# Gate matrices of an expert layer traced between the activations ahead of the value steps

## The chip, the cores and the metric

The kernel runs on one core of one Trainium2 chip. The metric is device time in microseconds (us) of one execution; several executions are timed and their median is given. In this document PE is TensorE, DVE is VectorE, ACT is ScalarE, POOL is GpSimd and SP is the engine whose queue issues most loads.

## The reference

Two layers work on 256 latent tokens and 256 context tokens of width 1024. Layer 0 mixes the tokens by a bidirectional mLSTM beside windowed attention, layer 1 by gated linear attention. After each mixer comes a retrieval layer over 128 x 128 = 16384 single-neuron experts, and the change is inside that layer:

```python
def block(hb):                                     # hb: 128 tokens
    q = (hb @ wq).reshape(tc, 8, 2, 128)
    s = jnp.einsum('thpk,hpnk->thpn', q, keys)
    s_top, i_top = lax.top_k(s, 16)
    cand = s_top[:, :, 0, :, None] + s_top[:, :, 1, None, :]
    cid = i_top[:, :, 0, :, None] * 128 + i_top[:, :, 1, None, :]
    best, pos = lax.top_k(cand.reshape(tc, 8, -1), 16)
    eid = jnp.take_along_axis(cid.reshape(tc, 8, -1), pos, -1)
    g = jax.nn.softmax(best, -1)
    act = jax.nn.gelu(jnp.einsum('td,thed->the', hb, u[eid]))
    return jnp.einsum('the,thed->td', g * act, v[eid])
```

Each token so has 8 x 16 = 128 chosen experts with a weight (gate) each. Layer 0 runs this for 512 tokens, layer 1 for the 256 latent tokens.

## The kernel before

**The expert layer is computed densely.** For a tile of 128 tokens the kernel does not gather rows of `u` and `v`; it multiplies the tokens with all 16384 rows of `u`, multiplies the result by a matrix of gates that is zero for experts that were not chosen, and multiplies that with all rows of `v`. (One of layer 0's four tiles goes the other way, by indirect loads on POOL's queue, during the value steps.) Layer 0 has three dense tiles (384 tokens), layer 1 two (256 tokens).

**Stages of a dense layer.** `top16` takes the 16 best keys of each head and finds the 16 best pairs; a `lookup` on DVE (tiles `rge`, `rpr`, `rsf`) turns their positions into two indices, and the three rows of `rabg` hold the first index, the second index and the gate of 128 slots per token. `slots` transposes them on PE (`abgT`) and ACT copies the result to `iT` and `gT`. `expand` builds the gate matrix of 8 tokens at a time (a group): DVE writes `oa` (first index equal to a counter), `eq` (second index equal to it) and two products `ob` (`eq` times the gate in two half-precision parts), PE multiplies `oa` by `ob` (16 matmuls in two PSUM tiles `G`), ACT copies `G` into `stg`, and after two groups ACT's queue writes 1 MB of `stg` to DRAM. A tile has 16 groups, so layer 0 has 48 and layer 1 has 32.

`stream` is the rest. Step n of the activations (`u_step`, 64 of them) has two halves; each loads 512 KB of `u`, splits it into a high part `uhi` (ACT, line 140) and a low part `ulo` (line 141, on POOL when the argument `n` of `halves` is true, else on DVE), does 24 matmuls on PE and takes a GELU on ACT (`act`, line 880). Step n of the values (`v_step`) loads gates back (`gin`), multiplies them into `act`, splits the product (`wh`, `wl`) and two blocks of `v`, and accumulates in PSUM (`F`). Layer 0 computes 32 activation steps ahead of the first value step, layer 1 computes 23; these are the early steps, and in them all low halves are POOL's.

**What sets the order.** A tile scheduler places the instructions of every engine's queue from the order in which the Python code creates them and from the buffers: three each of `uhi` and `ulo`, five loads (`wt`), three each of `oa` and `eq`, four of `ob`, six PSUM banks for `G`, two for `u`, two of `stg`, and one `rabg`. Queues run in order. In the code before, all groups of all tiles are created ahead of `stream`. The transposes of `slots` alone are pinned by a table: tile i's stand on PE behind the activation step that `TURNS` names (line 31).

```python
TURNS = ((10, 13, 17), (7, 17))
            w = self.halves(self.I["u"][l, 2 * n + j], [P, KD, P], early or (2 * n + j) % 3 == 2, "u")
                for tt in range(2):
                    self.expand(self.slots(self.top16(route[tt])), gd, tt, count)
```

Of the kernel before, what the change touches and what calls it, by code (L numbers as in the profile page):

```python
# [9 lines left out]
F32 = mybir.dt.float32  # L10
# [10 lines left out]
P = 128  # L21
D = 1024
KD = 8
T = 256
# [3 lines left out]

STARTS = [0, 16, 24, 29, 34, 37, 40, 43] + list(range(46, 54))

TURNS = ((10, 13, 17), (7, 17))
NCAND = 54
GS = 2.0 ** 15

TG = 16
OT = 8
CH = 8
TD = 384
# [66 lines left out]
class Kernel:  # L105
# [609 lines left out]
    def top16(self, route):  # L715

        nc, pp = self.nc, self.pp
# [25 lines left out]
            nc.vector.max_index(Px[:, h, 8:16], B[:, h, 8:16], C[:, h])  # L743
        pos = pp.tile([P, P], BF, name="rpos")
        nc.vector.tensor_copy(pos, Px.rearrange("t h k -> t (h k)"))
        abg = pp.tile([P, 3, P], F32, name="rabg")
        sf = pp.tile([P, P], BF, name="rsf")
        H = P // 2

# [48 lines left out]
    def expand(self, slots, gd, tt, count):  # L798

        nc = self.nc
        ix, gate = slots

        g = self.pp.tile([P, 2, P], F16, name="gpair")
        nc.vector.tensor_scalar(g[:, 0], gate, GS, None, op0=OP.mult)
        nc.vector.scalar_tensor_tensor(g[:, 1], gate, GS, g[:, 0], op0=OP.mult, op1=OP.subtract)
        for tg in range(P // TG):
            stg = self.sb("stg", [P, P, TG], "stg")
            for o in range(TG // OT):  # L810
                t0 = tg * TG + OT * o
                shape = [P, OT // 2, P, 2]
                oa = self.sb("s2a", shape, "oa", F16)
                eq = self.sb("s2b", shape, "eq", F16)
                ob = self.sb("rows", [P, 2] + shape[1:], "ob", F16)

                def each(x):
                    return x[:, t0:t0 + OT].rearrange("p (a t) -> p a t", t=2)[:, :, None, :].to_broadcast(shape)
                iota = count[:, None].to_broadcast(shape)
                nc.vector.tensor_tensor(oa, iota, each(ix[:, 0]), op=OP.is_equal)  # L820
                nc.vector.tensor_tensor(eq, iota, each(ix[:, 1]), op=OP.is_equal)  # L821
                for h in range(2):
                    nc.vector.tensor_tensor(ob[:, h], eq, each(g[:, h]), op=OP.mult)  # L823
                for j in range(OT // 4):
                    ps = self.bank([P, 4, P], "G")
                    for i in range(4):
                        a, t = divmod(4 * j + i, 2)
                        self.mm(ps[:, i], oa[:, a, :, t], ob[:, 0, a, :, t], True, False)
                        self.mm(ps[:, i], oa[:, a, :, t], ob[:, 1, a, :, t], False, True)
                    c = OT * o + 4 * j  # L830
                    nc.scalar.copy(stg[:, :, c:c + 4].rearrange("p i t -> p t i"), ps)  # L831
            nc.scalar.dma_start(gd[:, :, tt * (P // TG) + tg].rearrange("b p c t -> p b (c t)"),
                                stg.rearrange("p (b c) t -> p b (c t)", c=CH))

    def gather_start(self, abg):

# [34 lines left out]
    def u_step(self, l, n, c0, nt, early):  # L871

        nc = self.nc
        a = self.sb("ring", [P, 2, nt], "act")
        for j in range(2):
            w = self.halves(self.I["u"][l, 2 * n + j], [P, KD, P], early or (2 * n + j) % 3 == 2, "u")
            ps = self.bank([P, nt], "u", "u")
            for k in range(KD):
                i = self.mm3(ps, [x[:, k] for x in w], self.hcols(k, c0, nt), k == 0, k == KD - 1)
            nc.scalar.activation(a[:, j], ps, AF.Gelu)  # L880

        for t, tile_no in self.turns:
            if TURNS[l][tile_no] == n:
                self.tc.add_manual_dep(t, i.ins.name, mybir.DependencyInfo(
                    mybir.DependencyClass.NoSync, mybir.DependencyReason.DATA), reason="issue order")
        return a
# [32 lines left out]
                self.mm(F[tt][hf], w[:, j, ts], b[:, hf * 512:hf * 512 + 512],  # L919
                        first and w is wh and b is hi, last and w is wl)  # L920

    def stream(self, l, gd, c0, nt, ahead, spill, side=None):


        nc = self.nc
# [3 lines left out]
            order += [("u", x), ("v", x - ahead + spill)]  # L929
        order += [("v", y) for y in range(64 - ahead + spill, 64)]  # L930
        acts, far = {}, {}
        for i, (what, n) in enumerate(order):
            if what == "u":
                a = self.u_step(l, n, c0, nt, n < ahead)
                if n < spill:
# [377 lines left out]
    def run(self):  # L1313
# [4 lines left out]
        with self.banks("S"):  # L1318
            with self.open("S"):
                F = self.experts0()  # L1320
# [3 lines left out]
        with self.banks("S"):  # L1324
            with self.open("S2"):
                gd = self.pd.tile([P // CH, P, T // TG, CH, TG], F32, name="G1")
# [1 line left out]
                weave((self.route(1, "l", route), 16))  # L1328
                self.turns, self.tile_no = [], 0
                count = self.count()  # L1330
                for tt in range(2):
                    self.expand(self.slots(self.top16(route[tt])), gd, tt, count)
                mods = self.seq(self.modulation(1, 5, (0,), "stg"), self.last_rows(xd["l"]))
                F = self.stream(1, gd, T, T, 23, 0, lambda x: x >= 35 and x % 8 == 3 and next(mods, None))
                self.last_norm(F)

    def experts0(self):
# [3 lines left out]
        route = []  # L1341
# [2 lines left out]
        gst = self.gst = self.gather_start(self.top16(self.route_c[0]))  # L1344
        slots = [self.slots(self.top16(r)) for r in self.route_c[1:] + route]
        count = self.count()
        for tt in range(3):
            self.expand(slots[tt], gd, tt, count)
        gst["f"] = self.sb("fa", [P, D], "fa")
        nc.gpsimd.memset(gst["f"], 0.0)  # L1350
        gst["rows"], done, far, spill = {}, [0, 0], 4, 28
# [3 lines left out]
        def side(x):  # L1355
# [7 lines left out]
            while done[1] < goal:  # L1363
# [2 lines left out]
                    done[0] += 1  # L1366
                self.gather_use(gst, done[1])
                done[1] += 1
        return self.stream(0, gd, P, TD, 32, spill, side)

    def mixers(self, xd):
        nc, pw, I = self.nc, self.pw, self.I
# [156 lines left out]
```

## Time and profile before

| what | value |
|---|---|
| median of 3 timed runs | 2882.25 us (2881.95 to 2882.57) |
| profiled execution | 2876.07 us, span of its instructions 2874.2 us |
| PE busy | 2677.6 us (93%) |
| DVE busy | 2118.8 us (74%) |
| POOL busy | 1373.0 us (48%) |
| ACT busy | 1269.8 us (44%) |
| bytes moved by DMA | 644.36 MB, mean 224 GB/s |

Busy shares are averages over stages with different limits. In this profile the activations of layer 0 begin at about 521 us, its value steps run from 891 to 1700 us, layer 1's activations begin at about 2035 us and its value steps run from 2277 us to the end. A busy PE is not always a PE at its peak, so a stage is read by its matmul counts beside its length.

### The profile page before, as it was taken

How to read it: one execution, taken by the hardware profiler on the slowest of the kernel's cores; microseconds unless marked ns; L12 is line 12 of the kernel's file. 1: busy time of each engine (PE TensorE's matmuls, PEld its weight loads, DVE VectorE, ACT ScalarE, POOL GpSimd, SP SyncE). 2: the span in 40 equal slices, each digit the busy share in tenths (PEclk: the TensorE clock that was granted, in tenths of full speed). 3: DMA queues.
4: the chain of work that ended last, by engine and by line, in shares of the span. 5: the costliest groups of instructions: out<-in, count | busy, mean ns of one | idle time of the engine just before them, and what ended most of it. 6: DMA issues, size and time to landing. Idle time of an engine off the chain costs nothing. (4 is left out here: it accounts for less than half of the span.)

```text
span 2874.2 us, 42060 instructions
## 1 busy us (share of the span) xinstructions
PE 2677.6 (93%) x15935; PEld 2394.7 (83%) x15935; DVE 2118.8 (74%) x3686; ACT 1269.8 (44%) x1867; POOL 1373.0 (48%) x644
## 2 busy tenths in 40 slices
PE   7998898998789999999999988988988899999998
PEld 5787898998788888988989876778987799999986
DVE  7979758958755878788988887865899765444445
ACT  2234545435663333333333326544465544444454
POOL 1121346565666556777777752235756432222221
PEclk8999999999899999999999999999999999999999
DMA  7644223445788989999988972223465886666564
GB/s 273 199 161 140 95 96 134 172 174 168 233 265 304 350 341 391 348 329 346 341 329 327 344 262 86 81 81 118 162 199 175 270 304 220 214 204 213 183 198 136
DMA packets 243387, 644.36 MB, mean 224 GB/s; under 512 B 19536, under 2 KB 101456, under 8 KB 237808
## 3 DMA queue, kind: packets, MB, share of 16 engines
q1 hardware_dynamic: 119728, 454.48, 44.9%
q0 software_dynamic: 36864, 134.23, 12.9%
q10 hardware_dynamic: 86592, 52.96, 5.9%
q8 instruction: 125, 2.05, 0.3%
q14 instruction: 78, 0.64, 0.1%
HBM read 583.40 MB, written 58.20 MB: 223 GB/s over the span
## 5 line engine op out<-in xcount | busy, mean ns | idle before, releaser
L141 POOL TENSOR_TENSOR ulo<-wt,uhi 128x1024 fp32r<-128x1024 f32 x158 | 490.9, 3113 | 481.2 <-ACT uhi L140 468.1
L165 PE MATMUL u<-hh,ulo 128*128 128x384 f32 (+1 forms) x2048 | 642.7, 314 | 29.0 <-POOL ulo L141 27.4
L165 PE MATMUL u<-hh,uhi 128*128 128x384 f32 (+1 forms) x2048 | 644.4, 315 | 21.0 <-ACT act L880 16.1
L165 PE MATMUL u<-hl,uhi 128*128 128x384 f32 (+1 forms) x2048 | 641.7, 313 | 0.0
L165 PE MATMUL F<-vlo,wh 128*128 128x512 f32 x1280 | 462.5, 395 | 1.2 <-DVE vlo L141 1.2
L140 ACT CAST uhi<-wt 128x1024 fp32r<-128x1024 f32 x256 | 268.7, 1050 | 408.0 <-issue 138.7
L141 POOL TENSOR_TENSOR wlo<-wt,whi 128x1024 fp32r<-128x1024 f32 (+2 forms) x96 | 235.9, 2461 | 444.0 <-ACT whi L140 386.5
L165 PE MATMUL F<-vhi,wh 128*128 128x512 f32 x1280 | 438.0, 395 | 3.4 <-ACT wh L140 3.4
L165 PEld LDWEIGHTS u<-hh,ulo 128*128 128x128 f32 x2048 | 395.0, 193 | 31.2 <-POOL ulo L141 29.1
L165 PEld LDWEIGHTS u<-hh,uhi 128*128 128x128 f32 x2048 | 395.5, 193 | 26.5 <-ACT act L880 17.1
L165 PE MATMUL F<-vhi,wl 128*128 128x512 f32 x1280 | 402.2, 395 | 0.0
L165 PEld LDWEIGHTS u<-hl,uhi 128*128 128x128 f32 x2048 | 395.1, 193 | 3.4
L140 ACT CAST vhi<-wt 128x1024 fp32r<-128x1024 f32 x256 | 268.2, 1049 | 257.6 <-issue 105.1
L141 POOL TENSOR_TENSOR vlo<-wt,vhi 128x1024 fp32r<-128x1024 f32 x82 | 210.5, 2566 | 269.1 <-ACT vhi L140 230.7
L141 DVE TENSOR_TENSOR vlo<-wt,vhi 128x1024 fp32r<-128x1024 f32 x174 | 219.6, 1263 | 127.3 <-ACT vhi L140 127.2
L165 PEld LDWEIGHTS F<-vhi,wl 128*128 128x128 f32 x1280 | 241.3, 189 | 56.1
L165 PEld LDWEIGHTS F<-vhi,wh 128*128 128x128 f32 x1280 | 240.5, 189 | 55.8 <-ACT wh L140 3.8
L165 PEld LDWEIGHTS F<-vlo,wh 128*128 128x128 f32 x1280 | 240.7, 189 | 55.1 <-DVE vlo L141 1.7
L140 ACT CAST whi<-wt 128x1024 fp32r<-128x1024 f32 (+2 forms) x122 | 124.3, 1022 | 259.5 <-issue 62.9
L854 POOL DMA_INDIRECT rows<-in_v_dram,giv x128 | 189.5, 1481 | 97.5 <-DVE fa L869 63.0
L252 DVE SCALAR_TENSOR_TENSOR junk<-wt,silr 128x1024 bf16<-128x1024 f32 x144 | 209.0, 1451 | 29.9 <-DMA wt<-in_wmodt_dram 28.5
L854 POOL DMA_INDIRECT rows<-in_u_dram,giv x128 | 195.2, 1525 | 62.9 <-DVE rows L866 34.9
(382 smaller groups left out, 4851.0 us busy)
## 6 DMA issues: line engine op xcount, KB each, us to landing
wt<-in_u_dram SPq DMA_DIRECT2D x256, 512.0 KB
wt<-in_v_dram SPq DMA_DIRECT2D x256, 512.0 KB
wt<-in_wmodt_dram SPq DMA_DIRECT2D x88, 512.0 KB
G<-stg ACTq DMA_DIRECT2D x40, 1024.0 KB
wt<-in_wq_dram SPq DMA_DIRECT2D x48, 512.0 KB
gin<-G SPq DMA_DIRECT2D x16, 1536.0 KB
gin<-G SPq DMA_DIRECT2D x16, 1024.0 KB
far<-act ACTq DMA_DIRECT2D x28, 384.0 KB
```

The lines of the kernel that those rows point to most:

```text
L140: self.nc.scalar.copy(hi, src)
L141: i = (self.nc.gpsimd if n else self.nc.vector).tensor_sub(lo, src, hi.bitcast(F32))
L165: return self.nc.tensor.matmul(out, lhsT=lhsT, rhs=rhs, start=start, stop=stop, **kw)
L252: nc.vector.scalar_tensor_tensor(junk, w, 1.0, self.silr[:, i], op0=OP.mult, op1=OP.mult, accum_out=m[:, k, i:i + 1])
L854: self.nc.gpsimd.indirect_dma_start(out=rows, out_offset=None, in_=src, in_offset=bass.IndirectOffsetOnAxis(ap=idx[:, j:j + 1], axis=0))
```

## The change

1. `TURNS` moves the transposes: layer 0 from behind steps 10, 13, 17 to 9, 12, 15; layer 1 from 7, 17 to 5, 8.
2. `rabg` has two buffers in place of one, so the lookup of one tile may write while the transposes of the tile before have not read theirs.
3. `expand` is now a generator that yields after each group; `stream` draws from it. From activation step 15 on (layer 0) 3.5 groups are created per step, and from step 9 on (layer 1) 3 groups per step, ahead of the step's own code; what is left is drawn ahead of the first value step. Layer 1 makes the slots of both tiles first.
4. Low halves of `u` in early steps are POOL's only below step 15 (layer 0) or 9 (layer 1); in the early steps from there on they are DVE's.

```diff
-TURNS = ((10, 13, 17), (7, 17))
+TURNS = ((9, 12, 15), (5, 8))
+
+SPREAD = ((15, 3.5), (9, 3))
...
-        abg = pp.tile([P, 3, P], F32, name="rabg")
+        abg = pp.tile([P, 3, P], F32, name="rabg", bufs=2)
...
                     nc.scalar.copy(stg[:, :, c:c + 4].rearrange("p i t -> p t i"), ps)
+                if o < TG // OT - 1:
+                    yield
             nc.scalar.dma_start(gd[:, :, tt * (P // TG) + tg].rearrange("b p c t -> p b (c t)"),
                                 stg.rearrange("p (b c) t -> p b (c t)", c=CH))
+            yield
...
-            w = self.halves(self.I["u"][l, 2 * n + j], [P, KD, P], early or (2 * n + j) % 3 == 2, "u")
+
+            w = self.halves(self.I["u"][l, 2 * n + j], [P, KD, P],
+                            n < SPREAD[l][0] if early else (2 * n + j) % 3 == 2, "u")
...
-    def stream(self, l, gd, c0, nt, ahead, spill, side=None):
+    def stream(self, l, gd, c0, nt, ahead, spill, spread, side=None):
...
+        begin, groups, given = *SPREAD[l], 0
         for i, (what, n) in enumerate(order):
+            if what == "v" and n == 0:
+                for _ in spread:
+                    pass
+            if what == "u" and begin <= n < ahead:
+                while given < groups * (n + 1 - begin) and next(spread, self) is not self:
+                    given += 1
             if what == "u":
                 a = self.u_step(l, n, c0, nt, n < ahead)
...
-                for tt in range(2):
-                    self.expand(self.slots(self.top16(route[tt])), gd, tt, count)
+                slots = [self.slots(self.top16(r)) for r in route]
+                spread = self.seq(*[self.expand(slots[tt], gd, tt, count) for tt in range(2)])
                 mods = self.seq(self.modulation(1, 5, (0,), "stg"), self.last_rows(xd["l"]))
-                F = self.stream(1, gd, T, T, 23, 0, lambda x: x >= 35 and x % 8 == 3 and next(mods, None))
+                F = self.stream(1, gd, T, T, 23, 0, spread, lambda x: x >= 35 and x % 8 == 3 and next(mods, None))
...
-        for tt in range(3):
-            self.expand(slots[tt], gd, tt, count)
+        spread = self.seq(*[self.expand(slots[tt], gd, tt, count) for tt in range(3)])
...
-        return self.stream(0, gd, P, TD, 32, spill, side)
+        return self.stream(0, gd, P, TD, 32, spill, spread, side)
```

What this does to the queues is shown at three places. The first is DVE in layer 0, in the run of gate matrices behind the last lookup, before (`oa`, `eq`, `ob` are the three kinds of gate instructions):

```order
L765 TENSOR_REDUCE rabg<-rpr 128x64 x2
L820 TENSOR_TENSOR oa<-count,iT 128x1024
L823 TENSOR_TENSOR ob<-eq,gpair 128x1024 x2
L820 TENSOR_TENSOR oa<-count,iT 128x1024
L823 TENSOR_TENSOR ob<-eq,gpair 128x1024 x2
L821 TENSOR_TENSOR eq<-count,iT 128x1024
L820 TENSOR_TENSOR oa<-count,iT 128x1024
L823 TENSOR_TENSOR ob<-eq,gpair 128x1024 x2
L821 TENSOR_TENSOR eq<-count,iT 128x1024
```

And the same place with the change, some instructions further on, once the run has begun:

```order
L825 TENSOR_TENSOR ob<-eq,gpair 128x1024 x4
L143 TENSOR_TENSOR ulo<-wt,uhi 128x1024
L823 TENSOR_TENSOR eq<-count,iT 128x1024
L822 TENSOR_TENSOR oa<-count,iT 128x1024
L823 TENSOR_TENSOR eq<-count,iT 128x1024 x2
L822 TENSOR_TENSOR oa<-count,iT 128x1024
L143 TENSOR_TENSOR ulo<-wt,uhi 128x1024
L825 TENSOR_TENSOR ob<-eq,gpair 128x1024 x2
L822 TENSOR_TENSOR oa<-count,iT 128x1024
L825 TENSOR_TENSOR ob<-eq,gpair 128x1024 x4
```

Low halves of `u` now stand between the gate instructions on DVE. POOL, which had 64 low halves in a row here, has 30 and then goes on to the value steps. On PE the first gate matmul moves from behind activation half 35 to behind half 31, and the last from behind half 52 to behind half 55 (halves counted from 0).

The second place is ACT in layer 0, at the exponential of the third tile's gates (`rabg<-rabg`), with the table load ahead of it; before it stood behind the transposed indices of the tile before and activation step 10 (`far_10`):

```order
L140 CAST uhi<-wt 128x1024
L880 ACTIVATE act<-u 128x384
L788 CAST iT<-abgT 128x256
L789 COPY gT<-abgT 128x128
L770 ACT_TABLE_LOAD
L770 ACTIVATE rabg<-rabg 128x128
L937 DMA far_10_7448<-act 128x768
L140 CAST uhi<-wt 128x1024
L880 ACT_TABLE_LOAD
```

With the change it stands at step 3:

```order
L142 CAST uhi<-wt 128x1024
L887 ACTIVATE act<-u 128x384
L772 ACT_TABLE_LOAD
L772 ACTIVATE rabg<-rabg 128x128
L951 DMA far_3_5626<-act 128x768
L142 CAST uhi<-wt 128x1024
L887 ACT_TABLE_LOAD
L887 ACTIVATE act<-u 128x384
```

The exponential of the tile after it moves in the same way, from step 14 to step 9, right behind the first tile's transposed indices.

The third place is DVE in layer 1, in the first tile's lookup. Before, the second tile's best pairs (`rB`, `rP`, `rC`) came after the first tile's gate matrices:

```order
L765 TENSOR_REDUCE rabg<-rpr 128x64
L765 TENSOR_REDUCE rsf<-rpr 128x64
L778 TENSOR_TENSOR rabg<-rabg,rden 128x128
L761 TENSOR_TENSOR rpr<-rge,rD 128x1024
L759 TENSOR_TENSOR rpr<-rge,rtb 128x1024
L765 TENSOR_REDUCE rabg<-rpr 128x64
L765 TENSOR_REDUCE rsf<-rpr 128x64
L773 TENSOR_TENSOR rpos<-rpos,rsf 128x128
```

With the change they stand between the instructions of the first tile's lookup:

```order
L767 TENSOR_REDUCE rabg<-rpr 128x64
L767 TENSOR_REDUCE rsf<-rpr 128x64
L743 MATCH_REPLACE rC<-rB,rC 128x54
L744 MAX rB<-rC 128x8 x2
L743 MATCH_REPLACE rC<-rB,rC 128x54 x5
L780 TENSOR_TENSOR rabg<-rabg,rden 128x128
L763 TENSOR_TENSOR rpr<-rge,rD 128x1024
L761 TENSOR_TENSOR rpr<-rge,rtb 128x1024
L744 MAX rB<-rC 128x8
L745 MAX_INDEX rP<-rB,rC 128x8 x2
L744 MAX rB<-rC 128x8 x5
```

In layer 1 the gate matmuls on PE begin behind half 147 in place of 146 (layer 1's halves are 128 to 255), and the last ones stand behind half 176 in place of inside half 175; one half, 177, is left between them and the first value matmul.

## Rows read from the trace of the kernel before

**Rows 1.** Busy time by stretch: PE, weight loads, DVE, ACT, POOL, clock, DMA share, GB/s.
```profile
694.00:842.00 148.00, 124.29 (x1172) 116.78 (x1171) 117.86 (x178) 109.27 (x128) 101.22 (x17) 0.91 0.75 235
891.00:1700.00 809.00, 805.73 (x3852) 703.44 (x3851) 685.75 (x680) 276.12 (x324) 549.05 (x316) 1.00 0.92 340
2042.00:2277.00 235.00, 190.16 (x1695) 184.28 (x1694) 203.30 (x345) 132.61 (x175) 141.41 (x46) 0.93 0.61 195
```

**Rows 2.** PE's waits, 640 to 880 us: total us, times, longest.
```profile
PE u L165 <- POOL ulo L141: 23.3, 3, 8.0
PE abgT L785 <- DVE rabg L765: 6.9, 1, 6.9
```

**Rows 3.** PE's waits, 2040 to 2290 us.
```profile
PE G L165 <- DVE ob L823: 17.4, 11, 5.6
PE abgT L785 <- DVE rabg L765: 8.4, 1, 8.4
PE u L165 <- ACT act L880: 7.1, 2, 5.3
```

**Rows 4.** POOL's timeline, 680 to 770 us: start, us, instruction, idle before.
```profile
686.64 2.39 POOL L141 TENSOR_TENSOR ulo<-wt,uhi 128x1024 fp32r<-128x1024 f32 x1 [1.74 <-ACT uhi L140]
690.80 2.39 POOL L141 TENSOR_TENSOR ulo<-wt,uhi 128x1024 fp32r<-128x1024 f32 x1 [1.77 <-ACT uhi L140]
704.92 26.91 POOL L141 TENSOR_TENSOR ulo<-wt,uhi 128x1024 fp32r<-128x1024 f32 x3 [7.58 <-PE G L165]
```

**Rows 5.** DVE's timeline at the same time.
```profile
705.64 0.68 DVE L820 TENSOR_TENSOR oa<-count,iT 128x1024 f16<-128x1024 f16 x1
706.24 0.68 DVE L821 TENSOR_TENSOR eq<-count,iT 128x1024 f16<-128x1024 f16 x1
```

**Rows 6.** PE's instructions, 694 to 842 us: count, busy us, mean ns, idle before.
```profile
L165 PE MATMUL G<-ob,oa 128*128 128x128 f16 x768 | 53.2, 223 | 0.5 <-DVE oa L820 0.5
L165 PE MATMUL u<-hh,ulo 128*128 128x384 f32 x131 | 47.8, 365 | 23.3 <-POOL ulo L141 23.3
```

**Rows 7.** PE's instructions, 2042.6 to 2277.2 us.
```profile
L165 PE MATMUL u<-hh,ulo 128*128 128x256 f32 x390 | 114.9, 295 | 5.4 <-POOL ulo L141 3.9 <-DVE ulo L141 1.5
L165 PE MATMUL G<-ob,oa 128*128 128x128 f16 x512 | 42.8, 232 | 17.7 <-DVE ob L823 17.4
```

**Rows 8.** PE's timeline: one block of gate matmuls.
```profile
704.23 2.06 PE L165 MATMUL G<-ob,oa 128*128 128x128 f16 x32
```

**Rows 9.** DVE's waits, 590 to 700 us.
```profile
DVE rabg L769 <- PE abgT L785: 29.6, 1, 29.6
```

**Rows 10.** ACT's instructions, 694 to 842 us.
```profile
L831 ACT COPY stg<-G 128x512 f32<-128x512 f32 x92 | 87.5, 1102 | 34.5 <-PE G L165 29.1 <-DMA G<-stg 4.3 <-ACT stg L831 0.5
```

**Rows 11.** ACT's timeline in layer 1.
```profile
2047.79 1.05 ACT L140 CAST uhi<-wt 128x1024 fp32r<-128x1024 f32 x1 [1.55 <-issue]
2050.67 1.05 ACT L140 CAST uhi<-wt 128x1024 fp32r<-128x1024 f32 x1 [1.55 <-issue]
```

**Rows 12.** DVE's instructions, 2042 to 2265 us.
```profile
L823 DVE TENSOR_TENSOR ob<-eq,gpair 128x1024 f16<-128x1024 f16 x64 | 59.9, 977 | 5.7 <-PE G L165 5.5
L820 DVE TENSOR_TENSOR oa<-count,iT 128x1024 f16<-128x1024 f16 x32 | 32.3, 1009 | 4.1 <-ACT iT L788 4.1
L754 DVE TENSOR_TENSOR rge<-rpos,rtb 128x1024 bf16<-128x1024 bf16 x8 | 16.0, 2037 | 0.1
L761 DVE TENSOR_TENSOR rpr<-rge,rD 128x1024 bf16<-128x1024 bf16 x8 | 15.9, 2010 | 0.0
L759 DVE TENSOR_TENSOR rpr<-rge,rtb 128x1024 bf16<-128x1024 bf16 x4 | 11.5, 2884 | 0.0
L141 DVE TENSOR_TENSOR ulo<-wt,uhi 128x1024 fp32r<-128x1024 f32 x2 | 2.4, 1219 | 10.9 <-ACT uhi L140 10.9
```

**Rows 13.** PE's timeline at the end of layer 1's gate matmuls.
```profile
2259.95 1.22 PE L165 MATMUL G<-ob,oa 128*128 128x128 f16 x14
2277.20 0.56 PE L165 MATMUL F<-vhi,wh 128*128 128x512 f32 x1 [3.36 <-ACT wh L140]
```

## What the change was predicted to do

> **What bounds the kernel now.** I read the busy times by stretch first [rows 1]: in layer 0's value steps PE works 805.7 of 809 us, so nothing is to be had there, and the change doesn't touch them. In the stretch where layer 0's gate matrices are made (694 to 842 us) PE works only 124 of 148 us at a granted clock of 0.91, and in layer 1 ahead of the value steps (2042 to 2277 us) 190 of 235 us at 0.93. Those two stretches hold what can be won. Next come PE's waits in them. In layer 0 they are few and long: 23.3 us in three waits for a low half that POOL makes, and 6.9 us for a lookup [rows 2]. In layer 1 they are many and short and mostly DVE's: 17.4 us in 11 waits for `ob`, 8.4 us for the lookup, 7.1 us for ACT's `act` [rows 3].
>
> The timeline of POOL beside that of DVE shows why its low halves come late. One takes 2.39 us while DVE does other things, but the three that begin at 704.92 take 26.91 us [rows 4], just while DVE runs gate instructions back to back, one every 0.60 us (706.24 − 705.64 [rows 5]). So POOL and DVE can't both work at speed there. If the last two of the three took 2.39 each, the first took 26.91 − 4.78 = 22 us, so it was held for some 20 us, or 33 gate instructions of 0.60.
>
> The Trainium skill, page "SBUF — State Buffer", section "Who interferes with whom", says that DVE and GpSimd share a port pair that is locked for a whole instruction, the other engine then being fully blocked. The trace agrees on the blocking, but a lock given up after each instruction would cost a low half 0.7 us and not 20; by that alone layer 0 would give back about 3 × 0.7 = 2 us.
>
> **How long the stretches would be without waits.** Layer 0's halves follow each other every 4.16 us at full clock (690.80 − 686.64 [rows 4]). A half has 8 matmuls with `ulo`, so 131 of them are 16.4 halves, 68.1 us; 768 gate matmuls [rows 6] at 2.06/32 = 0.064 us [rows 8] are 49.4 us. That is 117.5 of 148 us: 30.5 us lost, 23.8 in waits and the rest with the lower clock. With the lookup's 6.9 us [rows 2] 37.4 us can go. Layer 1's halves take 2.88 us (2050.67 − 2047.79 [rows 11]); 390/8 = 48.75 halves and 512 gate matmuls [rows 7] are 140.4 + 32.8 = 173 us of 234.6, 61 us lost. But the last gate matmuls end at about 2261 and the first value matmul starts at 2277.20 [rows 13]: ACT's copy, the write, the load back and the product `wh` take those 16 us, of which the change takes away nothing, as it leaves one or two halves behind the last group, as before. So at most 61 − 17 = 44 us.
>
> **Layer 0, part by part.** *Low halves to DVE, groups between the halves.* The POOL waits go, since POOL has no low halves from step 15 on, where the gate instructions begin. What is late next? Per step DVE now has 3.5 groups × 4 × 0.60 = 8.4 us and two lows of 1.22 [rows 12] = 10.8 us. PE has 2 × 4.16 + 3.5 × 16 × 0.064 = 11.9. ACT has 7 copies of 0.95 (87.5/92 [rows 10]), two `uhi` and two `act`, about 11 us by an estimate of 1.0 to 1.1 us for each of the latter [rows 11]. All three are within a tenth or so, PE the longest, so the stage is bounded by PE with little slack. Queues run in order and DVE's lows stand between gate instructions, so I leave 4 us for it (0 to 20). *Earlier transposes, two `rabg`.* DVE's wait of 29.6 us for `abgT` [rows 9] goes, so the lookups run earlier, and PE's 6.9 us with it. In return two exponentials stand earlier in ACT's queue, at steps 3 and 9; ACT waits there for the sum that a lookup needs, and behind it stand `uhi` and `act`, so PE would wait. No row shows this; from below it is nothing, from above it is about the 8.0 us that the longest wait of PE took here [rows 2]. I take 4. *Loads.* The stretch moves 235 GB/s at a DMA share of 0.75; in 30 us less it would move about 295, and the value steps move 340 [rows 1], so the queues carry it. Last group to first value step: eight halves, 33 us, stand between, which covers the 16 us. Sum: −37.4 + 4 + 4 = −29 us, bounds −10 and −37.
>
> **Layer 1.** There DVE bounds: 203.3 of 235 us busy [rows 1], PE waiting for `ob`. Steps have 3 × 4 × 0.60 + 2 × 1.22 = 9.6 us on DVE against 2 × 2.88 + 48 × 0.064 = 8.8 us on PE. So I add up DVE's own work:
> - 28 low halves more (steps 9 to 22, two each), × 1.22 [rows 12]: +34 us.
> - The 64 `ob` and 32 `oa` take 59.9 + 32.3 = 92.2 us [rows 12], against 96 × 0.60 = 57.6 where POOL is held off [rows 5]. POOL does no low halves beside them any more: −34.6 us.
> - `rge` and the products `rpr` of the lookups take 16.0 + 15.9 + 11.5 = 43.4 us for 20 instructions [rows 12]. At 1.2 for `rge` (as a low half) and 0.60 for the others they are 16.8: 26.6 us too long. POOL's early lows go on beside the first lookup and not beside all of the second; I take half: −13.
> - DVE's idle time of 5.7 us ahead of `ob`, 4.1 ahead of `oa` and 10.9 ahead of its lows [rows 12] can partly be filled with the other kind of work, as both now alternate. I take −7 of 20.7.
> - The second tile's best pairs stand inside the first lookup now, so `rabg` of the first tile comes later on DVE by a few us and the earlier `TURNS` makes PE wait longer for it than 8.4 us [rows 3]. That wait is in DVE's chain already and isn't counted twice.
>
> Sum: −21 us. From one side: all of the lookups' excess and all idle time go, which is more than the 44 us that PE allows; I take −44. From the other: the gate instructions stay as slow as now (POOL wasn't the cause) and 20.7 us of idle time are filled: +34 − 20.7 = +13.
>
> The Trainium skill, page "Perfetto Trace Analysis", section "Optimizing Scalar/DVE Operations", speaks against this part: if DVE is saturated, it says, some work may be worth moving to Scalar or even GPSIMD. Here work goes the other way, onto the busiest waited-for engine. By that page layer 1 would come out near the +13 above. The same paragraph notes that the two share a read port, so that a move between them might not help.
>
> **The sum.** 2876.07 − 29 − 21 = 2826 us for the profiled execution. The median of the runs stands 6.2 us above it (2882.25 − 2876.07): 2832 us.
>
> **The rivals.**
> 1. *The stalls come back on DVE's or ACT's order in layer 0.* For it: three engines at 11 to 12 us per step, queues in order, ACT's exponentials. Against: the value steps show queues of this sort running at 99.6% of PE [rows 1]. Half of layer 0 returns: 2847.
> 2. *Layer 1 gives nothing.* DVE pays the lows and gets the excess back only in part. For it: DVE is the engine waited for [rows 3] and 34 us are added to it; `ob` is slow there by an average, with PE's own waits mixed in. Against: rows 4 and 5 show the two engines in each other's way. 2853, and with +13 it is 2866. This is also the page's case.
> 3. *Better than forecast*: both lookups are freed, and layer 0 loses nothing on ACT: −37 − 35 gives 2810.
> 4. *DVE and PE alternate* (the slower side). A half's `ulo` stands in DVE's queue behind an `ob`; that `ob` needs a free one of four buffers, so a gate matmul on PE, and that stands behind the half before, which needs its own `ulo`. If this loop closes, PE doesn't work while DVE makes gates. Fully in turn it costs 48/3.5 × 10.8 = 148 us in layer 0 and 32/3 × 9.6 = 102 in layer 1. The gain of 50 is gone when a fifth of these 250 us isn't hidden; at a third it is 2832 + 83 = 2915. Against: three `ulo` and four `ob` let DVE be a half and two groups ahead.
> 5. *It doesn't do what it says*: PE's waits in layer 0 have another cause that stays, and DVE's sum in layer 1 is even. 2882.
>
> **Chances.** Forecast 0.50 (own range 2818 to 2842), rival 1 0.15, rival 2 0.13, rival 3 0.11, rival 4 0.06, rival 5 0.05. A measurement of this kernel can tell about 0.2%, 6 us, from no change. Faster: 0.50 + 0.15 + 0.13 + 0.11 = 0.89; the same 0.05; slower 0.06. The range from 2806 to 2862 holds the forecast, rivals 1 and 3 and most of 2.
>
> **What would show it.** Right, in layer 0: no wait of PE for POOL's `ulo` ahead of 842 us, POOL's low halves back at 2.4 us, and the first value matmul some 29 us earlier than 891. In layer 1: `ob` and `oa` at about 0.6 to 0.7 us, fewer and shorter waits for `ob`, and still 16 us between the last gate matmul and the first value matmul. Wrong: PE waiting for DVE's `ulo` or `ob` at every step (rival 4); long waits for `act` near steps 3 and 9 behind an exponential (rival 1); `ob` near 0.95 though POOL rests (rival 2). It would be refuted if value steps changed by more than a few us, as the whole forecast lies in two stretches.

## The result, and the profile after

| | before | after |
|---|---|---|
| median of 4 runs | 2882.14 us (2881.95 to 2882.57) | 2831.15 us (2827.48 to 2831.38) |
| profiled execution | 2876.07 us | 2831.02 us |
| span of its instructions | 2874.2 us | 2829.2 us |

The ratio is 0.982 (95% interval 0.9806 to 0.9834): 51 us less. The forecast was 2832 us, with a range of 2806 to 2862.

The two traces, cut where PE's work changes its kind (first and last matmul of a kind):

| stretch | before, us | after, us | change |
|---|---|---|---|
| start to first activation of layer 0 | 521.3 | 526.3 | +5.0 |
| layer 0, first activation to first value matmul | 369.8 | 331.5 | −38.3 |
| layer 0, value steps | 811.9 | 811.1 | −0.8 |
| to first activation of layer 1 | 331.8 | 328.3 | −3.5 |
| layer 1, first activation to first gate matmul | 72.4 | 85.2 | +12.8 |
| layer 1, first to last gate matmul | 153.7 | 127.9 | −25.8 |
| layer 1, last gate matmul to first value matmul | 16.2 | 16.9 | +0.7 |
| layer 1, value steps | 586.0 | 591.1 | +5.1 |
| rest | 11.0 | 10.9 | −0.1 |
| span | 2874.2 | 2829.2 | −45.0 |

The first row lies ahead of everything that the change touches. The first activation of layer 0 starts between 521.3 and 530.1 us in the traces of before, after and the ten experiments, so those 5 us are told apart from the rest: without them the stretches give −49.9 us.

Busy time by stretch after (PE, weight loads, DVE, ACT, POOL, granted clock, DMA share, GB/s): layer 0's gates, its value steps, layer 1 ahead of its value steps.

```profile
681.00:828.00 147.00, 147.00 (x1341) 142.70 (x1340) 133.34 (x203) 119.41 (x144) 0.00 (x0) 1.00 0.91 278
858.00:1668.00 810.00, 806.23 (x3860) 703.32 (x3859) 692.18 (x684) 276.33 (x324) 547.52 (x318) 1.00 0.92 344
1997.00:2227.00 230.00, 193.00 (x1757) 188.13 (x1755) 199.99 (x410) 136.86 (x184) 52.05 (x20) 0.92 0.65 207
```

Against [rows 1], PE is busy in every microsecond of layer 0's gate stretch, at a clock of 1.00 in place of 0.91, and POOL does nothing there. The stretch has the same length as before, but 192 `ulo` matmuls (24 halves) stand in it in place of 131. DVE (133 of 147 us) is close behind, as it was worked out. Layer 1 still has 37 us in which PE doesn't work.

PE's instructions in the first of these stretches (count, busy us, mean ns, idle before), to be held against [rows 6]:

```profile
L167 PE MATMUL u<-hh,ulo 128*128 128x384 f32 x192 | 64.7, 337 | 0.0
L167 PE MATMUL G<-ob,oa 128*128 128x128 f16 x761 | 49.8, 220 | 0.0
```

PE's waits after, 515 to 860 us (total us, times, longest):

```profile
PE u L167 <- ACT act L887: 10.3, 3, 6.8
```

and 1990 to 2240 us:

```profile
PE u L167 <- ACT act L887: 14.1, 4, 6.7
PE F L167 <- ACT wh L142: 11.4, 1, 11.4
PE u L167 <- DVE ulo L143: 7.7, 3, 6.2
PE G L167 <- DVE ob L825: 1.9, 3, 1.4
...
PE abgT L787 <- DVE rabg L767: 0.7, 1, 0.7
```

In layer 0 both rows of [rows 2] are gone. In layer 1 the 17.4 us for `ob` and the 8.4 us for the lookup [rows 3] have shrunk to 1.9 and 0.7. What has grown is ACT's `act`, from 7.1 to 14.1 us, DVE's `ulo`, from 1.5 [rows 7] to 7.7, and the wait for `wh` ahead of the first value matmul, from 3.36 [rows 13] to 11.4.

DVE's instructions after, 1997 to 2211 us, which answer to [rows 12]:

```profile
L825 DVE TENSOR_TENSOR ob<-eq,gpair 128x1024 f16<-128x1024 f16 x64 | 44.8, 739 | 7.3 <-PE G L167 7.3
L143 DVE TENSOR_TENSOR ulo<-wt,uhi 128x1024 fp32r<-128x1024 f32 x30 | 36.5, 1218 | 2.5 <-ACT uhi L142 2.2
L822 DVE TENSOR_TENSOR oa<-count,iT 128x1024 f16<-128x1024 f16 x32 | 21.7, 682 | 0.3
...
L756 DVE TENSOR_TENSOR rge<-rpos,rtb 128x1024 bf16<-128x1024 bf16 x8 | 13.8, 1761 | 0.0
L763 DVE TENSOR_TENSOR rpr<-rge,rD 128x1024 bf16<-128x1024 bf16 x8 | 10.4, 1318 | 0.0
...
L761 DVE TENSOR_TENSOR rpr<-rge,rtb 128x1024 bf16<-128x1024 bf16 x4 | 4.9, 1230 | 0.0
```

`oa` and `ob` are down from 92.2 to 66.5 us. The longer `act` waits are seen on ACT's timeline (start, us, instruction, idle before):

```profile
2017.22 1.28 ACT L772 ACT_TABLE_LOAD   x1
2025.40 0.31 ACT L772 ACTIVATE rabg<-rabg 128x128 f32<-128x128 f32 x1 [6.89 <-DVE rabg L771]
2025.61 1.03 ACT L142 CAST uhi<-wt 128x1024 fp32r<-128x1024 f32 x1
...
2039.96 1.28 ACT L772 ACT_TABLE_LOAD   x1
2047.48 0.31 ACT L772 ACTIVATE rabg<-rabg 128x128 f32<-128x128 f32 x1 [6.24 <-DVE rabg L771]
2047.70 1.03 ACT L142 CAST uhi<-wt 128x1024 fp32r<-128x1024 f32 x1
```

The exponentials of both tiles' gates wait at the head of ACT's queue until DVE has found the best pairs. `uhi` and `act` of the activations stand behind them, and PE waits for `act`, 6.7 us at the longest.

### The profile page after: what moved, and what is told of

The parts are those of the page before. It is cut to its first block, busy times and chain, and to the rows that moved or that the text cites. A ratio compares the mean times of both kernels' runs of the same rounds, so it can differ in the third digit from the quotient of the medians.

```text
span 2829.2 us, 42059 instructions
## 1 busy us (share of the span) xinstructions
PE 2664.5 (94%) x15935; PEld 2385.5 (84%) x15935; DVE 2149.6 (76%) x3748; ACT 1267.6 (45%) x1867; POOL 1125.4 (40%) x582
## 3 DMA queue, kind: packets, MB, share of 16 engines
q0 software_dynamic: 36864, 134.23, 12.8%
## 5 line engine op out<-in xcount | busy, mean ns | idle before, releaser
L143 POOL TENSOR_TENSOR ulo<-wt,uhi 128x1024 fp32r<-128x1024 f32 x96 | 245.5, 2558 | 476.8 <-ACT uhi L142 474.1
L167 PEld LDWEIGHTS u<-hh,ulo 128*128 128x128 f32 x2048 | 392.5, 192 | 11.1 <-DVE ulo L143 10.2
L143 DVE TENSOR_TENSOR vlo<-wt,vhi 128x1024 fp32r<-128x1024 f32 x174 | 227.9, 1310 | 123.1 <-ACT vhi L142 123.0
L143 DVE TENSOR_TENSOR ulo<-wt,uhi 128x1024 fp32r<-128x1024 f32 x160 | 202.2, 1265 | 132.7 <-ACT uhi L142 132.5
L167 PEld LDWEIGHTS F<-vhi,wh 128*128 128x128 f32 x1280 | 240.7, 189 | 65.4 <-ACT wh L142 13.3
L254 DVE SCALAR_TENSOR_TENSOR junk<-wt,silr 128x1024 bf16<-128x1024 f32 x144 | 202.5, 1406 | 23.3 <-DMA wt<-in_wmodt_dram 22.0
```

Of the source, the lines that this page charges most:

```text
L143: i = (self.nc.gpsimd if n else self.nc.vector).tensor_sub(lo, src, hi.bitcast(F32))
L167: return self.nc.tensor.matmul(out, lhsT=lhsT, rhs=rhs, start=start, stop=stop, **kw)
L254: nc.vector.scalar_tensor_tensor(junk, w, 1.0, self.silr[:, i], op0=OP.mult, op1=OP.mult, accum_out=m[:, k, i:i + 1])
```

## Experiments

Each kernel ran beside the kernel before. A ratio is to that kernel, with its 95% interval; "layer 0" and "layer 1" are the stretches from the first activation to the first value matmul, 331.5 and 230.0 us in the changed kernel. The kernel before had medians of 2879 to 2882 us beside the different groups of runs, so a difference between medians of two rows, or of a row and the changed kernel, is good to about 3 us. In mix, pool_l1 and best1 layer 1 has 24 early steps and not 23: their last column holds one step more (5.8 us), and their value steps one less.

| run | median, us | ratio | layer 0 | layer 1 |
|---|---|---|---|---|
| lows_pool | 2861.01 | 0.9942 (0.9926 to 0.9958) | 352.6 | 234.2 |
| no_spread | 2837.76 | 0.9858 (0.9843 to 0.9873) | 335.9 | 231.7 |
| layer0_only | 2837.54 | 0.9861 (0.9844 to 0.9878) | 329.3 | 244.3 |
| one_rabg | 2847.43 | 0.9893 (0.9878 to 0.9908) | 336.6 | 236.2 |
| lazy | 2832.57 | 0.9843 (0.9828 to 0.9858) | 332.0 | 236.1 |
| exp_late | 2821.45 | 0.9798 (0.9785 to 0.9811) | 325.9 | 226.4 |
| mix | 2825.83 | 0.9818 (0.9804 to 0.9831) | 318.8 | 242.5 |
| pool_l1 | 2821.54 | 0.9792 (0.9778 to 0.9807) | 320.4 | 235.7 |
| best0 | 2818.09 | 0.9783 (0.9767 to 0.9799) | 321.5 | 226.3 |
| best1 | 2810.90 | 0.9758 (0.9741 to 0.9774) | 318.8 | 224.0 |

**lows_pool: the lows stay POOL's, the groups are spread.**

```diff
-                            n < SPREAD[l][0] if early else (2 * n + j) % 3 == 2, "u")
+                            True if early else (2 * n + j) % 3 == 2, "u")
```

> The changed kernel, but all low halves of early activation steps are POOL's again; the groups stay spread. Theory A (what left is POOL being held off by gate instructions, so the move of the lows to DVE carries the gain): with 3.5 groups per step DVE runs gate instructions for 8.4 of 11.9 us, so POOL's lows in layer 0 stay long (5 to 10 us each), PE waits for POOL's ulo as before, layer 0's first value matmul comes 15 to 35 us later than in the changed kernel (872 to 893 us of the trace) and the median is 2855 to 2890. Theory B (spreading the groups carries it, POOL finds its turn between them): lows of 2.4 to 3.5 us, hardly a wait of PE for POOL, median within 10 us of 2831.

Measured: 2861.01 us, layer 0 21.1 us longer, so theory A, though POOL's 25 lows beside the gates took 4.13 us in the mean and not 5 to 10. POOL's and DVE's timelines of this run at one place (start, us, instruction):

```profile
772.99 20.36 POOL L143 TENSOR_TENSOR ulo<-wt,uhi 128x1024 fp32r<-128x1024 f32 x3 [3.50 <-ACT uhi L142]
```

```profile
772.98 0.68 DVE L822 TENSOR_TENSOR oa<-count,iT 128x1024 f16<-128x1024 f16 x1
773.58 1.28 DVE L825 TENSOR_TENSOR ob<-eq,gpair 128x1024 f16<-128x1024 f16 x2
...
784.76 1.28 DVE L825 TENSOR_TENSOR ob<-eq,gpair 128x1024 f16<-128x1024 f16 x2
786.07 2.72 DVE L823 TENSOR_TENSOR eq<-count,iT 128x1024 f16<-128x1024 f16 x1
```

The first low begins within a run of gate instructions that DVE issues back to back, and POOL's three lows take 20.36 us together. At 786.07 the picture turns: one `eq` takes 2.72 us, where its like take 0.68. So the low gets its turn when the run of DVE ends, and then DVE's next instruction is held instead. What that costs DVE is seen in its gate instructions of layer 0, in this run (676 to 848 us):

```profile
L825 DVE TENSOR_TENSOR ob<-eq,gpair 128x1024 f16<-128x1024 f16 x88 | 71.5, 852 | 0.0
L822 DVE TENSOR_TENSOR oa<-count,iT 128x1024 f16<-128x1024 f16 x45 | 40.0, 891 | 30.9 <-PE G L167 30.8
L823 DVE TENSOR_TENSOR eq<-count,iT 128x1024 f16<-128x1024 f16 x41 | 37.0, 932 | 0.1
```

and in the changed kernel (681 to 828 us), where DVE makes the lows too:

```profile
L825 DVE TENSOR_TENSOR ob<-eq,gpair 128x1024 f16<-128x1024 f16 x88 | 55.6, 683 | 0.0
L822 DVE TENSOR_TENSOR oa<-count,iT 128x1024 f16<-128x1024 f16 x45 | 30.6, 684 | 4.3 <-PE G L167 4.3
L143 DVE TENSOR_TENSOR ulo<-wt,uhi 128x1024 fp32r<-128x1024 f32 x25 | 30.5, 1220 | 12.3 <-ACT uhi L142 12.3
L823 DVE TENSOR_TENSOR eq<-count,iT 128x1024 f16<-128x1024 f16 x41 | 26.9, 683 | 0.0
```

The 25 lows cost DVE 30.5 us, but the same 174 gate instructions take it 113.1 us in place of 148.5. In this stage the move takes work from POOL and adds none to DVE. PE's waits of lows_pool, 640 to 880 us, show what is left of the old stalls:

```profile
PE u L167 <- POOL ulo L143: 10.6, 3, 4.5
PE G L167 <- DVE oa L822: 2.1, 1, 2.1
```

Without the lows' move, the rest of the change (spread groups, two `rabg`, earlier transposes) cuts the 23.3 us of [rows 2] to 10.6. In layer 1 the lows' move is worth 4.2 us (234.2 − 230.0).

**no_spread: all groups created ahead of the activations, lows on DVE.**

```diff
         begin, groups, given = *SPREAD[l], 0
+        for _ in spread:
+            pass
```

> The changed kernel, but all groups are created ahead of the first activation step, as before the change; the lows from step 15 (9) on stay on DVE. Theory A (the move carries the gain): since the order of DVE's queue still has lows between gate instructions, PE's waits for POOL stay away and the median is 2828 to 2842. Theory B (spreading carries it): lows stand late behind runs of gate instructions, PE waits for DVE's ulo at many steps, the median is 2860 to 2890.

Measured: 2837.76 us, layer 0 4.4 us longer, layer 1 1.7. Theory A: DVE's queue has the lows between the gates in this kernel too, since the scheduler puts them there, and PE waits for POOL nowhere in layer 0. The share of the spreading by itself is some 6 us.

**layer0_only: layer 1 as before.**

```diff
-TURNS = ((9, 12, 15), (5, 8))
+TURNS = ((9, 12, 15), (7, 17))
-SPREAD = ((15, 3.5), (9, 3))
+SPREAD = ((15, 3.5), (99, 3))
...
-                slots = [self.slots(self.top16(r)) for r in route]
-                spread = self.seq(*[self.expand(slots[tt], gd, tt, count) for tt in range(2)])
+                for tt in range(2):
+                    for _ in self.expand(self.slots(self.top16(route[tt])), gd, tt, count):
+                        pass
+                spread = iter(())
```

> The changed kernel in layer 0; layer 1 as before the change (tables, POOL's lows, slots of the second tile behind the first tile's groups), with two rabg. By the two traces layer 0 gave 38 us from the first activation to the first value matmul and layer 1 gave 12, of which 5 went again in the value steps: theory A expects 2831 + 7 to 12 = 2838 to 2843, with 242 us in layer 1 from the first activation to the first value matmul. The rival (layer 1's part is worth what was forecast, 21 us, and the first comparison of the traces understates it) expects 2850 to 2854.

Measured: 2837.54 us, 6.4 more than the changed kernel; layer 1 takes 244.3 us (242 expected), its value steps 587.0 against 591.1. By the trace layer 1's part is worth 14.3 − 4.1 = 10.2 us, by the medians 6.4, both far from 21. The median falls just under the expected 2838 and well under the rival's 2850.

**one_rabg: points 1 and 2 undone.**

```diff
-TURNS = ((9, 12, 15), (5, 8))
+TURNS = ((10, 13, 17), (7, 17))
...
-        abg = pp.tile([P, 3, P], F32, name="rabg", bufs=2)
+        abg = pp.tile([P, 3, P], F32, name="rabg")
```

> The changed kernel with points 1 and 2 of the change undone: one rabg, and the transposes at the steps of before (10, 13, 17 and 7, 17). Theory A (the two buffers and the earlier transposes are nearly paid for by the waits of ACT that they bring): in layer 0 PE's wait for the lookup (7 to 9 us) comes back and the two waits for act near 577 and 630 us (1.5 and 2.3 us, some 4 to 6 with the clock) go, so layer 0 changes by +2 to +5 us; layer 1 by 0 to +10 through a wait for the second lookup; median 2831 to 2846. Rival (the two buffers are a leading part, since DVE's wait of 29.6 us goes with them): layer 0 is 15 us or more longer, median over 2850.

Measured: 2847.43 us, 1.4 above the range that theory A gave and under the rival's. Layer 0 grew by 5.1 us, and DVE has its wait of [rows 9] again:

```profile
DVE rabg L771 <- PE abgT L787: 29.6, 1, 29.6
```

29.6 us of DVE's waiting are worth 5.1 us of time in layer 0, since PE has activations to work on; it waits 3.0 us itself for a lookup there, not the 7 to 9 that were expected. Beside it stand 6.2 us in layer 1 and, unforeseen, 5.4 us in layer 0's value steps (816.5 against 811.1), where PE waits once 4.1 us for `wh`. The run lows_pool has 815.9 us there too, with 3.8 us for `wh` in two waits. Why these waits appear wasn't tried.

**lazy: in layer 1 the second tile's lookup after the first tile's groups.**

```diff
-                slots = [self.slots(self.top16(r)) for r in route]
-                spread = self.seq(*[self.expand(slots[tt], gd, tt, count) for tt in range(2)])
+                spread = self.seq(*[self.slotted(r, gd, tt, count) for tt, r in enumerate(route)])
...
+    def slotted(self, r, gd, tt, count):
+        yield from self.expand(self.slots(self.top16(r)), gd, tt, count)
```

> The changed kernel, but in layer 1 the second tile's best pairs, lookup and slots are created only after the first tile's 16 groups (transposes still at the earliest behind steps 5 and 8). Theory A (layer 1 won 26 us in its gate stretch and lost 13 before it, because the second tile's lookup now stands ahead of the first gate matrices): the stretch from the first activation to the first gate matmul falls from 85 to 70 to 76 us, but the lookup then interrupts DVE's lows and gates in the middle, and PE waits 10 to 30 us for ulo or abgT there: median 2828 to 2850. Rival (the early second lookup is the mistake, and late it is hidden): 2815 to 2822.

Measured: 2832.57 us, within theory A's range. The stretch ahead of the first gate matmul falls from 85.2 to 67.3 us, somewhat more than expected, the gate stretch grows from 127.9 to 152.4, layer 1 in all from 230.0 to 236.1. The lookup's cost can be moved, and where the change puts it is the better of the two places by 6 us in layer 1; its value steps give 3.6 of them back, and by the medians, 1.4 us apart, the two places can't be told from each other.

**exp_late: exponentials pinned on ACT behind later activations.**

```diff
+EXPS = ((None, 4, 6, 12), (5, 9))
...
-        nc.scalar.activation(abg[:, 2], abg[:, 2], AF.Exp)
+        self.exps.append(nc.scalar.activation(abg[:, 2], abg[:, 2], AF.Exp).ins)
...
-            nc.scalar.activation(a[:, j], ps, AF.Gelu)
+            act = nc.scalar.activation(a[:, j], ps, AF.Gelu)
...
+        for x, e in enumerate(self.exps):
+            if EXPS[l][x] == n:
+                self.tc.add_manual_dep(e, act.ins.name, mybir.DependencyInfo(
+                    mybir.DependencyClass.NoSync, mybir.DependencyReason.DATA), reason="issue order")
```

> The changed kernel with the exponentials of the gates pinned on ACT behind later activations: layer 0's three dense tiles behind steps 4, 6 and 12, layer 1's two behind steps 5 and 9, so that ACT does not wait there for DVE's best pairs with uhi queued behind. Theory A (these waits of ACT are what PE lost: 7.0, 1.5 and 2.3 us in layer 0, 6.9 and 5.3 in layer 1): 15 to 23 us less, median 2808 to 2816. Rival (the time is bounded by DVE's lookups and comes back as waits for abgT, ob or in the 17 us between the last gate matmul and the first value matmul): 2825 to 2835.

(`None` in `EXPS` leaves the exponential of the gathered tile where it was.)

Measured: 2821.45 us, 9.7 less: between the two. In layer 0 the 10.3 us for `act` are gone, but PE now waits 7.0 us once for DVE's `ulo`, which stands behind the third lookup. In layer 1, 1985 to 2280 us:

```profile
PE F L168 <- ACT wh L143: 17.5, 1, 17.5
PE abgT L788 <- DVE rabg L768: 12.0, 2, 11.1
PE abgT L788 <- DVE rabg L781: 4.3, 1, 4.3
...
PE u L168 <- ACT act L888: 1.0, 2, 0.8
```

The waits of ACT did stop PE: 14.1 us for `act` are down to 1.0. But the waits at the transposes are up from 0.7 to 16.3 us, and the one at the end grows by 6, so of layer 1 only 3.6 us come back.

**mix and pool_l1: layer 0's lows from step 16; in layer 1 half of the lows, or all, on POOL again.**

```diff
-TURNS = ((9, 12, 15), (5, 8))
+TURNS = ((9, 12, 15), (7, 9))
-SPREAD = ((15, 3.5), (9, 3))
+SPREAD = ((15, 3.5), (9, 4))
+LOWS = (16, 9)
...
-                            n < SPREAD[l][0] if early else (2 * n + j) % 3 == 2, "u")
+                            (n < LOWS[l] or l and j) if early else (2 * n + j) % 3 == 2, "u")
...
-                F = self.stream(1, gd, T, T, 23,
+                F = self.stream(1, gd, T, T, 24,
```

(mix; on top of exp_late. pool_l1 has `n < LOWS[l]` there and 99 for layer 1 in `LOWS`. Both have 25 buffers for layer 1's `act`.)

> The kernel with late exponentials (2821 us), and further: layer 0's lows go to DVE from step 16 and not 15; in layer 1 DVE makes only the first half's low of each step from step 9 on and POOL the second's, four groups per step, transposes behind steps 7 and 9, 24 early steps with 25 buffers for act. On PE the last gate matmul then stands 6 halves ahead of the first value matmul, not one. Theory A (layer 1's tail of 17 to 22 us after the last gate matmul and the waits for abgT are what is left): 7 us less in layer 0, 8 to 15 less in layer 1, median 2799 to 2808. Rival (POOL is held off by the gate instructions again, PE waits for POOL's ulo): layer 1 loses 5 to 20 us, median 2815 to 2835.

> As the run mix, but POOL makes all early lows of layer 1. Theory A: POOL is held off while DVE runs up to 5 us of gate instructions in a row, lows last 3.3 us and more in the mean, but in layer 1 the stretch of gates is bounded by DVE (2.41 us per group, 32 groups, 77 us) and ends some 10 halves ahead of the first value matmul: 2800 to 2815, near to mix. Rival (moving the lows to DVE is needed in layer 1 as in layer 0): 2825 or more.

Measured: 2825.83 us, the rival's, and 2821.54 us, between the two theories. Layer 0 gave 7.1 us in mix (325.9 to 318.8) and 5.5 in pool_l1. Layer 1 with its value steps, which evens out the added step, takes 815.6 us in exp_late and 828.6 in mix. PE's waits in layer 1 of mix:

```profile
PE u L169 <- POOL ulo L145: 26.0, 4, 7.6
PE abgT L789 <- DVE rabg L769: 11.8, 2, 8.2
```

With both engines making lows, POOL's are long again (3.97 us in the mean) and PE waits 26.0 us for them. With all lows on POOL (pool_l1) DVE's `oa`, `eq` and `ob` take 113.8 us in place of 86.3 in exp_late, PE waits 7.1 us for POOL and 14.3 for `ob`, and layer 1 with its value steps is 823.0 us. Both are worse than all on DVE, by 13.0 and 7.4 us. Since groups per step, transposes and early steps changed along with the lows, these are prices of the whole settings and not of the lows alone.

**best0 and best1: the good parts together.** best0 is exp_late with `LOWS = (16, 9)`; best1 moves layer 1's transposes too and adds a step (with 25 buffers for layer 1's `act`):

```diff
-TURNS = ((9, 12, 15), (5, 8))
+TURNS = ((9, 12, 15), (8, 10))
...
-                F = self.stream(1, gd, T, T, 23,
+                F = self.stream(1, gd, T, T, 24,
```

> The kernel with late exponentials, and layer 0's lows on DVE from step 16 instead of 15 (the groups still from 15), which took 7 us of waits for DVE's ulo out of layer 0 in the run mix; layer 1 as in the kernel with late exponentials (all lows from step 9 on DVE, which gave its shortest layer 1, 226 us). The stages add up: layer 0 319 and layer 1 226 us from first activation to first value matmul, median 2812 to 2817. Rival (layer 1's and layer 0's gains don't add): 2819 to 2826.

> As best0, with layer 1's transposes behind steps 8 and 10, and 24 early steps in layer 1. Theory A (PE's 16 us of waits for abgT in layer 1 are idle time and nothing else): layer 1 takes 216 to 222 us to its first value matmul, of which 5.8 are the added step's, its value steps 5.8 less, median 2800 to 2806. Rival (the gate matmuls start later by as much, and end as late as before, with 17 us of waiting behind them): 2810 to 2820.

Measured: 2818.09 and 2810.90 us (2805.35 to 2812.44). best0 is above its range by 1 us: the stages add in layer 1, and layer 0 is 2.5 us longer than expected. best1 has layer 1 at 224.0 us, 2 over theory A's 216 to 222, and its median in the rival's range; with waits of 6.3 and 6.0 us for `abgT` and 9.0 us at the end, not the rival's 17, about half of what was hoped for came. It beats both kernels: 0.9758 against the changed kernel's 0.982.

## Why the prediction was right, and where its parts were off

**The total, 2832 us against 2831.15,** hides errors of opposite sign: layer 0 gave 38.3 us (forecast 29), layer 1 with its value steps 12.4 − 5.1 = 7.3 (forecast 21), and the stretch between the layers 3.5 and the value steps of layer 0 0.8 that weren't forecast. Together 49.9, for 50. The parts missed by 9 and 14 us, so that the total fits to 1 us is luck.

**Bringing the profile to the median** by adding 6.2 us was luck too, and not a property of profiling: the profiled execution of after stands 0.1 us from its median. That of before was a quick one: the executions of that kernel beside all runs span 2875.44 to 2890.51 us. The forecast for the profiled execution itself, 2826, was 5 us short. The 5.0 us in the stretch ahead of layer 0's activations may be most of that; no trace of a slower execution of before shows it.

**Layer 0: the mechanism was right, two terms mis-sized.** The whole of it, from the first activation to the first value matmul, before and after (columns as in [rows 1]):

```profile
521.30:891.10 369.80, 330.24 (x2344) 321.67 (x2343) 261.82 (x604) 195.05 (x250) 221.87 (x64) 0.94 0.63 210
526.30:857.80 331.50, 321.25 (x2344) 315.69 (x2343) 293.35 (x638) 193.81 (x250) 74.96 (x30) 0.98 0.71 228
```

PE's idle time falls by 29.3 us, and the same 2344 matmuls take 9.0 us less at a mean clock of 0.98 in place of 0.94: together the 38.3. The 30.5 us of the gate stretch and the 6.9 us of the lookup went whole. "So I leave 4 us for it" (queues in order with little slack) measured 0: PE was busy in 147.00 of 147.00 us with DVE at 91%. ACT's exponentials, taken at 4, cost 3.5: 10.3 us in three waits for `act`, against the one that before has ahead of 640 us:

```profile
PE u L165 <- ACT act L880: 6.8, 1, 6.8
```

Besides these, a wait of 2.2 us for `act` behind the gate stretch went; the last 2 us or so would be the clock ahead of the gate stretch, where before has 0.50, the lower of its two levels, from 663.0 to 669.8 us, around the end of PE's wait for the lookup. lows_pool says that the move of the lows carries 21.1 of the 38.3 us; no_spread and one_rabg put 4.4 and 5.1 on the spreading and on points 1 and 2. These are each taken away from the whole, so they needn't add up to it.

**Layer 1: right in its direction, a third of its size.** Its stretch up to the first value matmul, before and after, and then the part of it ahead of the first gate matmul (same columns):

```profile
2034.80:2277.20 242.40, 197.36 (x1757) 191.49 (x1755) 208.70 (x381) 136.53 (x184) 146.54 (x48) 0.94 0.61 194
1997.10:2227.10 230.00, 192.90 (x1756) 188.03 (x1755) 199.99 (x410) 136.96 (x185) 51.95 (x20) 0.92 0.65 207
2034.80:2107.20 72.40, 61.45 (x497) 61.14 (x496) 65.35 (x161) 33.50 (x54) 55.71 (x22) 0.95 0.48 165
1997.10:2082.30 85.20, 66.54 (x500) 65.71 (x500) 80.82 (x250) 35.43 (x56) 45.38 (x18) 0.86 0.37 126
```

The working added up DVE's own time, and that can be followed: DVE's busy time falls by 8.7 us and its idle time by 3.7, together the 12.4. +34 for the lows came (36.5 − 2.4 = +34.1), and −13 for the lookups came (43.4 − 29.1 = −14.3); what else DVE does took some 3 us less.

*The step that failed most is the term of the gates:* −34.6 forecast, 92.2 − 66.5 = −25.7 measured. It took as price the 0.60 us from one start to the next and subtracted it from a sum of durations. One instruction lasts 0.68 us and two in a row 1.28, so 64 `ob` and 32 `oa` come to 62.7 us even with nothing in their way, and not to 57.6. Most of the rest is two pairs of `ob` that run beside low halves of POOL for later steps:

```profile
2188.27 2.41 POOL L143 TENSOR_TENSOR ulo<-wt,uhi 128x1024 fp32r<-128x1024 f32 x1 [121.98 <-ACT uhi L142]
2188.82 3.01 DVE L825 TENSOR_TENSOR ob<-eq,gpair 128x1024 f16<-128x1024 f16 x2 [0.96 <-PE G L167]
2197.66 4.17 POOL L143 TENSOR_TENSOR vlo<-wt,vhi 128x1024 fp32r<-128x1024 f32 x1 [6.98 <-ACT vhi L142]
2199.80 3.18 DVE L825 TENSOR_TENSOR ob<-eq,gpair 128x1024 f16<-128x1024 f16 x2 [0.21 <-PE G L167]
```

*The idle time* was to give 7 of 20.7 us and gave 3.7. The 10.9 us ahead of DVE's lows in [rows 12] lie behind the last gate instruction of before, so no gate work could fill them:

```profile
2252.36 1.28 DVE L823 TENSOR_TENSOR ob<-eq,gpair 128x1024 f16<-128x1024 f16 x2
2264.50 1.23 DVE L141 TENSOR_TENSOR ulo<-wt,uhi 128x1024 fp32r<-128x1024 f32 x1 [10.85 <-ACT uhi L140]
```

*Where PE waits* came out otherwise than was said. The wait at the transposes, which was to grow beyond 8.4 us, is 0.7. But the second tile's best pairs now lie ahead of the first gate matmul, and DVE is busy there for 80.8 us in place of 65.4. PE's idle time in that part grows from 11.0 to 18.7 us, 11.8 of them for `act` behind the two exponentials and 6.2 for a low behind the second lookup, and its work takes 5.1 us longer at a mean clock of 0.86 in place of 0.95. I had priced the exponentials in layer 0 and left them out of layer 1. exp_late shows that they aren't the cause by themselves: with their waits gone that part is 83.8 us long and not 85.2, since PE then waits at the transposes for the lookups, which are late. In the gate stretch PE's idle time falls from 26.1 to 5.2 us; behind the last gate matmul it is 13.3 us in place of 8.0, as less of PE's own work is left there.

**Layer 1's value steps grew by 5.1 us,** where no more than a few us either way were to be seen. PE waits 1.7 us there for `ulo` and 1.8 us for `vlo`, both DVE's; where the other 1.6 us come from is open. The runs have 585 to 593 us there; none was made to settle it.

**The rivals.** The second (layer 1 gives nothing) was nearer to layer 1 than the forecast: 7 of 21 us came. The third had layer 0 (−37), but layer 1 gave nothing like its −35. The Trainium skill's sentence on moving work off a saturated DVE ("Perfetto Trace Analysis", "Optimizing Scalar/DVE Operations") was a fair warning for layer 1, where the lows' move alone gave 4.2 us; it would have been wrong for layer 0, where it gave 21.1. Still, going back to POOL for half of layer 1's lows, with mix's other edits, was worse by 13 us. The fourth rival, DVE and PE in turn, did not show: 1.9 us of waits for `ob` and 7.7 for `ulo` in layer 1, none in layer 0. The fifth is out, as both waits of [rows 2] went.

**The signs named beforehand.** In layer 0 no wait for POOL, its last lows ahead of the gates at 2.62 us in the mean, and the first value matmul at 857.8 us, 33 earlier than 891. In layer 1 `oa` at 682 and `ob` at 739 ns, three waits for `ob` in place of 11, and 16.9 us behind the last gate matmul. All came, with `ob` slower than the 0.6 to 0.7 expected, and so did one of the signs of the first rival: 6.8 us for `act` behind an exponential in layer 0, which however was there before too.

## What to carry to other kernels

Where two engines hold each other off, try giving both kinds of work to one of them, even to the busy one: in layer 0 DVE took on 30.5 us of lows, and its gate instructions, no longer held, took 35.4 us less. It paid as long as another engine remained the longest in a step (layer 0); where DVE itself was the longest, little came of it (layer 1). Price work in one kind of time: a row adds durations, which overlap, and the distance between starts is shorter. Before idle time is counted as something to fill, look where it lies. For every step that is created earlier, look at the in-order queues of all engines that it touches: one exponential of 0.31 us at the head of ACT's queue waited 6.89 us there, and PE with it. And compare a forecast part by part; a sum can be right by errors that cancel.

## What was not expected of the hardware

A low on POOL is held through a whole run of DVE's instructions and not through one: 13 us, from 772.99 to 786, through some 20 gate instructions in lows_pool, as 20 us in the trace of before. The Trainium skill ("SBUF — State Buffer", "Who interferes with whom") has the lock held for one instruction at a time and the loser fully blocked. The traces agree that the loser is blocked, in both directions (the `eq` of 2.72 us), but the turn does not change hands between instructions that stand back to back. Where the groups are spread POOL gets in more often: its lows beside layer 0's gates took 4.13 us in the mean in lows_pool (25 of them), 6.07 in the kernel before (17).
